# Column mean of an 8192x8192 matrix: 8 MB instead of 4 MB tiles, three quarters of the sums on VectorE, and all loads ahead of the outputs

## The chip, the cores and the metric

The kernel runs on one core of a Trainium2 chip; the other cores are idle. The metric is the time of one execution in microseconds (us), as the median of several runs. The profile's span, from the first to the last instruction, is about 1.8 us shorter than the time of the same run. Names of engines: PE is TensorE (matmul), DVE is VectorE, SP is SyncE; SPq is SP's queue, on which every DMA of this kernel is issued in program order.

## The reference

```python
def setup_inputs():
    return {"x": np.random.randn(8192, 8192).astype(np.float32)}

def reference(x):
    return np.mean(x, axis=0)
```

The input is 268.4 MB and is read once. The output is 32 KB.

## The kernel before

The matrix is read in 64 tiles of 128 rows (4 MB, one row of 32 KB per partition), in five buffers. PE sums over the partitions: a matmul with a column of 1/8192 as the stationary operand adds a block of 512 columns into a row of PSUM. The 16 blocks lie in six PSUM banks, three to a bank, at partitions 0, 32 and 64, so that matmuls of three blocks run side by side (in the trace 32 of them end within 7.0 us, though one takes 0.6 to 1.1 us). An f32 matmul is two instructions in the trace. In the last tile each bank is copied to SBUF by DVE and sent out, in the same loop that issues the loads:

```python
    for i in range(ntile):
        last = i == ntile - 1
        ...                      # pieces: head, bank by bank in the last two tiles, else whole
        t = in_pool.tile([P, C], fp32, name=f"in{i}", tag="in")
        for b0, nb in pieces:
            lo, hi = b0 * BLK, (b0 + nb) * BLK
            nc.sync.dma_start(out=t[:, lo:hi], in_=xt[i][:, lo:hi])
            for b in range(b0, b0 + nb):
                cols = slice(b * BLK, (b + 1) * BLK)
                mm(b, t[:, cols], stop=last)
            if last:
                ...
                nc.vector.tensor_copy(out=out_sb[0:rows, chunk], in_=ps[q][0:rows, :])
                ...
                nc.sync.dma_start(out=dst, in_=src)
```

Of the kernel before, what the change touches and what calls it, by code (L numbers as in the profile page):

```python
# [1 line left out]

# [4 lines left out]

BUFS = 5
GPB = 3  # L10
N_SPLIT = 2
HEAD_SPLIT = True
PROBE = False


@with_exitstack
def kernel(
    ctx: ExitStack,
    tc: tile.TileContext,
    x: bass.AP,  # L20
    out: bass.AP,
):
    nc = tc.nc
    P = nc.NUM_PARTITIONS
    R, C = x.shape
    fp32 = mybir.dt.float32
    BLK = 512
    nblk = (C + BLK - 1) // BLK
    assert C % BLK == 0 and R % P == 0
    inv_r = 1.0 / float(R)  # L30
    ntile = R // P
    nbank = (nblk + GPB - 1) // GPB

    pieces_bank = []
    b0 = 0
    for q in range(nbank):
        nb = min(GPB, nblk - b0)
        pieces_bank.append((b0, nb))
        b0 += nb
    pieces_head = [(0, 1), (1, nblk - 1)] if HEAD_SPLIT else [(0, nblk)]  # L40

    in_pool = ctx.enter_context(tc.tile_pool(name="in_pool", bufs=BUFS))
    const_pool = ctx.enter_context(tc.tile_pool(name="const_pool", bufs=1))
    out_pool = ctx.enter_context(tc.tile_pool(name="out_pool", bufs=1))
    psum_pool = ctx.enter_context(tc.tile_pool(name="psum_pool", bufs=1, space=bass.MemoryType.PSUM))

    ones = const_pool.tile([P, 1], fp32)
    nc.vector.memset(ones, inv_r)  # L48

    ps = [psum_pool.tile([P, BLK], fp32, name=f"ps{q}", tag=f"ps{q}") for q in range(nbank)]  # L50
    for q in range(nbank):
        rows = 32 * (min(GPB, nblk - q * GPB) - 1) + 1
        if rows > 1:
            nc.vector.memset(ps[q][0:rows], 0.0)  # L54
    out_sb = out_pool.tile([P, nbank * BLK], fp32)

    if PROBE and R >= 64 and C >= 4096:
        pr = const_pool.tile([64, 4096], fp32)
        nc.gpsimd.dma_start(out=pr[32:64, :], in_=x[0:32, 0:4096])

    def g_out(b):
        q, r = divmod(b, GPB)
        return ps[q][32 * r : 32 * r + 1, :]

    started = [False] * nblk

    def mm(b, rhs, stop=False):
        nc.tensor.matmul(g_out(b), ones, rhs, start=not started[b], stop=stop)  # L68
        started[b] = True

    xt = x.rearrange("(n p) m -> n p m", p=P)

    for i in range(ntile):
        last = i == ntile - 1
        if i == 0:
            pieces = pieces_head
        elif i >= ntile - N_SPLIT:
            pieces = pieces_bank
        else:
            pieces = [(0, nblk)]  # L80
        t = in_pool.tile([P, C], fp32, name=f"in{i}", tag="in")
        for b0, nb in pieces:
            lo, hi = b0 * BLK, (b0 + nb) * BLK
            nc.sync.dma_start(out=t[:, lo:hi], in_=xt[i][:, lo:hi])  # L84
            for b in range(b0, b0 + nb):
                cols = slice(b * BLK, (b + 1) * BLK)
                mm(b, t[:, cols], stop=last)
            if last:
                q = b0 // GPB
                rows = 32 * (nb - 1) + 1  # L90
                chunk = slice(q * BLK, (q + 1) * BLK)
                nc.vector.tensor_copy(out=out_sb[0:rows, chunk], in_=ps[q][0:rows, :])  # L92
                src = out_sb[0 : 32 * nb, chunk].rearrange("(r p) c -> r p c", p=32)[:, 0, :]
                dst = out[b0 * BLK : (b0 + nb) * BLK].rearrange("(r c) -> r c", c=BLK)
                nc.sync.dma_start(out=dst, in_=src)  # L95


# [1 line left out]
_INS = ['x']  # L99
_OUTS = [((8192,), 'float32')]  # L100


# [23 lines left out]
```

## Time and profile before

| | before |
|---|---|
| time, median of 5 runs | 639.2 us (639.1 to 640.9) |
| span of the profiled run | 638.3 us |
| 268.4 MB at the 431 GB/s of the middle | 623 us |
| PE busy | 427.9 us (67%) |
| DVE busy | 6.6 us (1%) |

The page of the kernel before: in 40 slices of the span, the busy share of the DMA engines in tenths and the GB/s they moved; then the DMA queue that fetches instructions (packets, MB, share).

```profile
DMA  9999999999999999999999999999999999999993
GB/s 372 446 430 427 426 427 435 443 431 426 429 429 426 435 436 431 432 429 429 426 433 432 432 437 426 433 424 433 431 434 433 426 435 427 432 431 434 417 388 132
q8 instruction: 16, 0.26, 0.2%
```

The DMA engines are full in every slice but the last, and the rate is flat near 430 GB/s until the last three slices. Sixteen packets of 16 KB fetch instructions while the kernel runs.

The table of windows of the kernel before: start and end of the window, its length, then busy us and instructions of each engine, the clock granted to PE, the DMA share and GB/s.

```profile
core 0: us, PE busy (x) PEld busy (x) DVE busy (x) POOL busy (x), PEclk, DMA share, GB/s
24.00:580.00 556.00, 377.79 (x1824) 67.65 (x1821) 0.00 (x0) 0.00 (x0) 0.85 1.00 431
624.30:638.30 14.00, 6.65 (x20) 0.38 (x20) 2.74 (x4) 0.00 (x0) 0.60 0.40 133
```

The first row says what bounds the kernel: DMA 100% busy at 431 GB/s, PE two thirds busy. The second is the end: DMA only 40% busy for 14 us. PE's timeline shows the same in the middle (start, length, instruction, and in brackets the idle time before it and what ended it):

```profile
325.39 7.01 PE L68 MATMUL ps<-in,ones 128*1 128x512 f32 x32 [2.71 <-DMA in<-in_x_dram]
335.10 5.31 PE L68 MATMUL ps<-in,ones 128*1 128x512 f32 x32 [2.70 <-DMA in<-in_x_dram]
```

A tile comes every 9.71 us, PE needs 5.3 to 8.1 us for it (the two lines show 7.0 and 5.3) and then waits for the next.

The end in SP's timeline and, in the last line, on PE (kernel before):

```profile
622.43 0.83 SPq L95 DMA_DIRECT2D out_dram<-out_sb  x1
623.31 0.36 SPq L84 DMA_DIRECT2D in<-in_x_dram  x1
624.26 2.52 SPq L95 DMA_DIRECT2D out_dram<-out_sb  x2
626.83 0.40 SPq L84 DMA_DIRECT2D in<-in_x_dram  x1
630.23 0.70 SPq L95 DMA_DIRECT2D out_dram<-out_sb  x1
630.98 0.40 SPq L84 DMA_DIRECT2D in<-in_x_dram  x1
633.84 2.77 SPq L95 DMA_DIRECT2D out_dram<-out_sb  x2
633.72 1.86 PE L68 MATMUL ps<-in,ones 128*1 128x512 f32 x2 [0.66 <-DMA in<-in_x_dram]
```

Outputs (L95) and loads (L84) alternate. An output waits for a copy, which waits for PE, which waits for a load; the next load stands behind it. The last three loads leave at 623.3, 626.8 and 631.0 us, and the DMA engines run dry between them.

### The profile page before, as it was taken

To read this page: it belongs to the slowest core of one execution; us is meant where nothing else is said; L and a number is where in the kernel's file an instruction comes from. 1 tells how busy PE (TensorE), PEld (TensorE's weight loads), DVE (VectorE), ACT (ScalarE), POOL (GpSimd) and SP (SyncE) were. 2 spreads that over 40 slices of the span, in tenths; PEclk is the share of its full clock that TensorE was granted. 3 is DMA by queue.
4 is the path that set the end of the run, shared out by engine and by line. 5 is a ranking of instruction groups with operands and counts; after the bars stand their busy time and mean duration, and the time that the engine had idled before them with its cause. 6 is when DMAs were issued, how large, how long until landed. Compare 5 with 4: busy or idle time off the path is not lost.

```text
span 638.3 us, 4305 instructions
## 1 busy us (share of the span) xinstructions
PE 427.9 (67%) x2048; PEld 75.6 (12%) x2048; DVE 6.6 (1%) x12; POOL 0.2 (0%) x4
## 2 busy tenths in 40 slices
PE   3676775866667667667667576677586666675884
PEld 0111110111111111101111011111011111110110
DVE  1000000000000000000000000000000000000002
POOL 0000000000000000000000000000000000000000
PEclk9878878787888898878887987887878788978886
DMA  9999999999999999999999999999999999999993
GB/s 372 446 430 427 426 427 435 443 431 426 429 429 426 435 436 431 432 429 429 426 433 432 432 437 426 433 424 433 431 434 433 426 435 427 432 431 434 417 388 132
DMA packets 10849, 268.74 MB, mean 421 GB/s; under 512 B 1216, under 2 KB 1216, under 8 KB 2896
## 3 DMA queue, kind: packets, MB, share of 16 engines
q1 hardware_dynamic: 10832, 268.47, 98.2%
q8 instruction: 16, 0.26, 0.2%
q14 instruction: 1, 0.01, 0.0%
HBM read 268.44 MB, written 0.03 MB: 421 GB/s over the span
## 4 chain that ended last, share of the span: by engine, by line
DMA 83%; PE 15%; SPq 0%; DVE 0%; issue 0%
DMA in<-in_x_dram 83%; PE ps L68 15%; DVE out_sb L92 0%; SPq L95 0%; SPq L84 0%
## 5 line engine op out<-in xcount | busy, mean ns | idle before, releaser
L68 PE MATMUL ps<-in,ones 128*1 128x512 f32 x2048 | 427.9, 730 | 207.7 <-DMA in<-in_x_dram 204.0
L68 PEld LDWEIGHTS ps<-in,ones 128*1 128x1 f32 x2048 | 75.6, 95 | 558.2 <-issue 284.7
L92 DVE COPY out_sb<-ps 65x512 f32<-65x512 f32 (+1 forms) x6 | 4.1, 685 | 628.6 <-PE ps L68 628.6
L54 DVE MEMSET ps<- 65x512 f32 x5 | 2.4, 485 | 0.3
L110 POOL MEMSET const-bfloat16-1.0<- 128x1 bf16 x1 | 0.1, 101 | 0.0
L110 POOL MEMSET const-uint8-127<- 128x1 uint8 x1 | 0.1, 101 | 0.0
L110 POOL MEMSET const-float32-0.0<- 128x1 f32 x1 | 0.1, 98 | 0.2 <-issue 0.2
L110 POOL MEMSET const-float32-1.0<- 128x1 f32 x1 | 0.1, 98 | 0.0
L48 DVE MEMSET ones<- 128x1 f32 x1 | 0.1, 59 | 0.8 <-PEq L110 0.8
## 6 DMA issues: line engine op xcount, KB each, us to landing
in<-in_x_dram SPq DMA_DIRECT2D x61, 4096.0 KB, 41.7
in<-in_x_dram SPq DMA_DIRECT2D x10, 768.0 KB, 9.1
in<-in_x_dram SPq DMA_DIRECT2D x1, 3840.0 KB, 11.8
in<-in_x_dram SPq DMA_DIRECT2D x3, 256.0 KB, 16.1
out_dram<-out_sb SPq DMA_DIRECT2D x5, 6.0 KB
out_dram<-out_sb SPq DMA_DIRECT2D x1, 2.0 KB
```

Source lines behind the costliest of these rows:

```text
L48: nc.vector.memset(ones, inv_r)
L54: nc.vector.memset(ps[q][0:rows], 0.0)
L68: nc.tensor.matmul(g_out(b), ones, rhs, start=not started[b], stop=stop)
L92: nc.vector.tensor_copy(out=out_sb[0:rows, chunk], in_=ps[q][0:rows, :])
L110: nc = _bacc.Bacc("TRN2", target_bir_lowering=False, num_devices=1)
```

## The change

The intent: read 8 MB per DMA, as two rows (64 KB, contiguous) per partition; let DVE add 12 of the 16 column blocks of tiles 0 to 28 into an accumulator, and PE only 4; fold the accumulator into PSUM before tile 29; and in the last tile issue every load before the first output. Two buffers of 8 MB replace five of 4 MB. The core of the diff, with cuts (some lines are joined or shortened):

```diff
-BUFS = 5
+BUFS = 2
 GPB = 3
-N_SPLIT = 2
+NPE = 4
+NEND = 3
+ROWS_PER_PART = 2
...
+    x3 = x.rearrange("(n p two) m -> n p (two m)", p=P, two=rpp)
...
+        if not endgame:
+            nc.sync.dma_start(out=t, in_=x3[i])
+            for h in range(rpp):
+                for b in range(npe):
+                    mm(b, t4[:, h, b * BLK : (b + 1) * BLK])
+            for h in range(rpp):
+                if ndve:
+                    nc.vector.tensor_tensor(out=acc, in0=acc,
+                        in1=t4[:, h, npe * BLK :], op=mybir.AluOpType.add)
+            continue
+        if i == ntile - nend and ndve:
+            for j in range(ndve):
+                mm(npe + j, acc[:, j * BLK : (j + 1) * BLK])
...
         for b0, nb in pieces:
             ...
-            nc.sync.dma_start(out=t[:, lo:hi], in_=xt[i][:, lo:hi])
+                nc.sync.dma_start(out=t4[:, :, lo:hi], in_=x4[i][:, :, lo:hi])
+        for b0, nb in pieces:
             for b in range(b0, b0 + nb):
+                for h in range(rpp):
+                    mm(b, t4[:, h, ...], stop=(last and h == rpp - 1))
+                if last:
+                    ...
+                        flush_bank(q)        # copy and output DMA
```

Tile 29 is still loaded whole; tiles 30 and 31 come in pieces of three blocks, the very last ones of two, one and one.

More of the change, by code (lines that the diff above doesn't have):

```diff
@@ L7 @@
 from concourse._compat import with_exitstack
-BUFS = 5
+BUFS = 2
 GPB = 3
-N_SPLIT = 2
-HEAD_SPLIT = True
-PROBE = False
+NPE = 4
+NEND = 3
+ROWS_PER_PART = 2
 @with_exitstack
@@ L27 @@
     BLK = 512
-    nblk = (C + BLK - 1) // BLK
-    assert C % BLK == 0 and R % P == 0
+    assert C % BLK == 0
+    nblk = C // BLK
     inv_r = 1.0 / float(R)
-    ntile = R // P
+    rpp = ROWS_PER_PART
+    TR = rpp * P
+    if R % TR != 0:
+        rpp = 1
+        TR = P
+    assert R % TR == 0
+    ntile = R // TR
     nbank = (nblk + GPB - 1) // GPB
+    npe = min(NPE, nblk)
+    ndve = nblk - npe
+    nend = min(NEND, ntile)
     pieces_bank = []
-    b0 = 0
     for q in range(nbank):
-        nb = min(GPB, nblk - b0)
-        pieces_bank.append((b0, nb))
-        b0 += nb
-    pieces_head = [(0, 1), (1, nblk - 1)] if HEAD_SPLIT else [(0, nblk)]
+        b0 = q * GPB
+        pieces_bank.append((b0, min(GPB, nblk - b0)))
+    pieces_last = []
+    for idx, (b0, nb) in enumerate(pieces_bank):
+        if idx >= len(pieces_bank) - 2 and nb > 1:
+            pieces_last.append((b0, nb - 1))
+            pieces_last.append((b0 + nb - 1, 1))
+        else:
+            pieces_last.append((b0, nb))
     in_pool = ctx.enter_context(tc.tile_pool(name="in_pool", bufs=BUFS))
     const_pool = ctx.enter_context(tc.tile_pool(name="const_pool", bufs=1))
-    out_pool = ctx.enter_context(tc.tile_pool(name="out_pool", bufs=1))
     psum_pool = ctx.enter_context(tc.tile_pool(name="psum_pool", bufs=1, space=bass.MemoryType.PSUM))
@@ L48 @@
     nc.vector.memset(ones, inv_r)
+    acc = None
+    if ndve:
+        acc = const_pool.tile([P, ndve * BLK], fp32)
+        nc.vector.memset(acc, 0.0)
+    out_sb = const_pool.tile([P, nbank * BLK], fp32)
     ps = [psum_pool.tile([P, BLK], fp32, name=f"ps{q}", tag=f"ps{q}") for q in range(nbank)]
@@ L54 @@
             nc.vector.memset(ps[q][0:rows], 0.0)
-    out_sb = out_pool.tile([P, nbank * BLK], fp32)
-    if PROBE and R >= 64 and C >= 4096:
-        pr = const_pool.tile([64, 4096], fp32)
-        nc.gpsimd.dma_start(out=pr[32:64, :], in_=x[0:32, 0:4096])
+    started = [False] * nblk
+    stopped_in_bank = [0] * nbank
     def g_out(b):
@@ L63, in g_out @@
         return ps[q][32 * r : 32 * r + 1, :]
-    started = [False] * nblk
     def mm(b, rhs, stop=False):
@@ L69, in mm, with flush_bank @@
         started[b] = True
-    xt = x.rearrange("(n p) m -> n p m", p=P)
-    for i in range(ntile):
+    def flush_bank(q):
+        ng = min(GPB, nblk - q * GPB)
+        rows = 32 * (ng - 1) + 1
+        chunk = slice(q * BLK, (q + 1) * BLK)
+        nc.vector.tensor_copy(out=out_sb[0:rows, chunk], in_=ps[q][0:rows, :])
+        b0 = q * GPB
+        src = out_sb[0 : 32 * ng, chunk].rearrange("(r p) c -> r p c", p=32)[:, 0, :]
+        dst = out[b0 * BLK : (b0 + ng) * BLK].rearrange("(r c) -> r c", c=BLK)
+        nc.sync.dma_start(out=dst, in_=src)
@@ new lines @@
+    x3 = x.rearrange("(n p two) m -> n p (two m)", p=P, two=rpp)
+    x4 = x.rearrange("(n p two) m -> n p two m", p=P, two=rpp)
+    for i in range(ntile):
+        t = in_pool.tile([P, rpp * C], fp32, name=f"in{i}", tag="in")
+        t4 = t.rearrange("p (two m) -> p two m", two=rpp)
+        endgame = i >= ntile - nend
+        if not endgame:
[4 more added lines that the diff above has]
+            for h in range(rpp):
+                if ndve:
+                    nc.vector.tensor_tensor(
+                        out=acc,
+                        in0=acc,
+                        in1=t4[:, h, npe * BLK :],
+                        op=mybir.AluOpType.add,
+                    )
+            continue
+        if i == ntile - nend and ndve:
+            for j in range(ndve):
+                mm(npe + j, acc[:, j * BLK : (j + 1) * BLK])
@@ L74 @@
         last = i == ntile - 1
-        if i == 0:
-            pieces = pieces_head
-        elif i >= ntile - N_SPLIT:
+        if i == ntile - nend and nend > 2:
+            pieces = [(0, nblk)]
+        elif not last:
             pieces = pieces_bank
         else:
-            pieces = [(0, nblk)]
-        t = in_pool.tile([P, C], fp32, name=f"in{i}", tag="in")
+            pieces = pieces_last
         for b0, nb in pieces:
             lo, hi = b0 * BLK, (b0 + nb) * BLK
-            nc.sync.dma_start(out=t[:, lo:hi], in_=xt[i][:, lo:hi])
-            for b in range(b0, b0 + nb):
-                cols = slice(b * BLK, (b + 1) * BLK)
-                mm(b, t[:, cols], stop=last)
-            if last:
-                q = b0 // GPB
-                rows = 32 * (nb - 1) + 1
-                chunk = slice(q * BLK, (q + 1) * BLK)
-                nc.vector.tensor_copy(out=out_sb[0:rows, chunk], in_=ps[q][0:rows, :])
-                src = out_sb[0 : 32 * nb, chunk].rearrange("(r p) c -> r p c", p=32)[:, 0, :]
-                dst = out[b0 * BLK : (b0 + nb) * BLK].rearrange("(r c) -> r c", c=BLK)
-                nc.sync.dma_start(out=dst, in_=src)
+            if (b0, nb) == (0, nblk):
+                nc.sync.dma_start(out=t, in_=x3[i])
+            elif rpp == 1:
+                nc.sync.dma_start(out=t4[:, 0, lo:hi], in_=x4[i][:, 0, lo:hi])
+            else:
+                nc.sync.dma_start(out=t4[:, :, lo:hi], in_=x4[i][:, :, lo:hi])
@@ L99 @@
+        for b0, nb in pieces:
+            for b in range(b0, b0 + nb):
+                for h in range(rpp):
+                    mm(b, t4[:, h, b * BLK : (b + 1) * BLK], stop=(last and h == rpp - 1))
+                if last:
+                    q = b // GPB
+                    stopped_in_bank[q] += 1
+                    if stopped_in_bank[q] == min(GPB, nblk - q * GPB):
+                        flush_bank(q)
 _INS = ['x']
```

## The prediction

> **What bounds it now.** The DMA stream. Table of windows: from 24 to 600 us the DMA engines are 100% busy at 431 GB/s, PE 392 of 576 us, DVE never. The Trainium skill ("DMA: Bandwidth & Descriptors", Where 436 GB/s comes from) puts the ceiling at 435 GB/s; the trace is at 99% of it. In the timeline PE starts a 4 MB tile every 9.71 us and needs 5.3 to 8.1 us for it; in the wait list it waits 204 us for input. 268.4 MB at 432 GB/s are 621 us of the 638.3 us span; some 17 us lie outside the stream, most after 600 us (slices 39 and 40 of the page: 388 and 132 GB/s).
>
> **What the change moves.**
> - 12 of 16 column blocks of tiles 0 to 28 go from PE to DVE, as f32 adds of 128x6144. The Trainium skill ("VectorE: DVE Perf Modes", the TRN2 errata) gives (N+151)/0.96 ns for them: estimate 6.56 us each, 13.1 us per 8 MB tile; no trace here shows one yet. PE was not on the critical path, so relieving it gains nothing by itself.
> - 5 buffers of 4 MB become 2 of 8 MB. A tile loads in 19.42 us; its buffer is free about 13.4 us after landing; issue to first packet is about 1 us. The next load is queued 4 to 5 us before the running one ends, so the stream should not break. This is the thinnest margin.
> - 64 KB instead of 32 KB rows per partition: at most 0.4% less packet cost. PE instructions fall from 2048 to about 700, so the 16 KB instruction fetches, which delay single DMA engines about 1 us each, become fewer: 1.5 to 2 us less at the end.
> - Head: one 8 MB load, no small piece: 0.8 us gained.
> - Tail, the real gain: output DMAs now stand between the input pieces on the one SP queue and wait there for PE and DVE (SP's waits: 18.6 us on the copy). The last pieces are issued at 623.3, 626.8 and 631.0 us and the last lands at 633.7; without these waits about 628.7. The change issues every input before the first output: 5 us gained.
> - Costs: two 8 MB tiles instead of two 4 MB go in pieces; 768 KB take 1.88 us against 1.82 at full rate: 0.7 us lost. The last block needs 4 instead of 2 dependent PE passes, 0.85 us each at the low clock: 1.7 us lost. In the last three tiles PE needs 10 (warm) to 17 us per 8 MB, still under 19.4.
>
> **Sum.** 638.3 - 5 - 0.8 - 2 - (0 to 2) + 0.7 + 1.7: about 632 us of span, a time of 633 us: 1% faster, inside 2%. Range 629 to 639. Faster by over 2%: 0.04; within 2%: 0.91; slower: 0.05.
>
> **What would show it.** DMA 100% and 431 GB/s in the middle; DVE adds of 6.5 us, busy about 380 us; PE starts tiles every 19.4 us; SP's waits in the middle are on DVE and end 4 to 6 us before the running load lands; in the tail no input issue behind an output, last input landing near 627, then about 6 us of passes, copy and output.
>
> **What would make it wrong.** Slower adds, or a longer way from the add's end to the next DMA's first packet: above 19.4 us in all, each tile adds a bubble, and 1 us of it costs about 30 us. 64 KB rows that read slower. PE cold in the last tiles and falling behind the pieces, which would give the tail's gain back.

## The result, and the profile after

The changed kernel takes 632.08 us (median of 7 runs, 631.86 to 632.34) beside 639.53 us for the kernel before (13 runs, 639.11 to 641.09). The ratio is 0.988, with a 95% interval of 0.987 to 0.989. The kernel is 1.2% faster; the predicted 633.0 us and its range of 629 to 639 us hold.

The page of the changed kernel, the same lines, and the group of the adds (busy us, mean ns of one, idle before):

```profile
GB/s 399 420 445 424 441 399 466 404 457 428 437 441 424 445 424 453 412 454 412 457 407 457 408 453 412 453 412 450 416 449 416 449 416 449 416 453 412 406 414 249
q8 instruction: 5, 0.08, 0.1%
L109 DVE TENSOR_TENSOR acc<-acc,in 128x6144 f32<-128x6144 f32 x58 | 380.4, 6558 | 188.8 <-DMA in<-in_x_dram 187.8
```

The last two slices moved 414 and 249 GB/s instead of 388 and 132. (The slices in the middle go up and down more than before. A 64 KB packet seems to be counted in one slice, so single slices say less here than the window below.) The add takes 6558 ns. The Trainium skill ("VectorE: DVE Perf Modes", the TRN2 errata) gives (N+151)/0.96 ns, checked there for 512 and 2048 elements; as an estimate, that is 6557 ns for 6144 elements, and the trace agrees.

The table of windows of the changed kernel:

```profile
24.00:580.00 556.00, 167.76 (x464) 23.67 (x463) 379.10 (x58) 0.00 (x0) 0.63 1.00 434
585.00:625.80 40.80, 31.31 (x190) 6.53 (x188) 2.75 (x4) 0.00 (x0) 1.00 0.98 398
```

In the middle the stream is as full as before, at 434 instead of 431 GB/s. PE's work has more than halved, and that is not where the time came from: PE was not the bound. The Trainium skill ("DMA: Bandwidth & Descriptors", Where 436 GB/s comes from) names 435 GB/s as the ceiling of the SBUF ports through which a core's DMA engines write; the trace comes within 0.3% of it. The same section lets a limit of about 358 GB/s on the HBM's side bind for loads from HBM; this trace, of one core with the others idle, lies well above that.

SP's timeline of the changed kernel, followed by the last matmuls on PE and the last add and copies on DVE:

```profile
579.31 30.97 SPq L135 DMA_DIRECT2D in<-in_x_dram  x13
612.14 16.63 SPq L93 DMA_DIRECT2D out_dram<-out_sb  x6
620.81 1.91 PE L82 MATMUL ps<-in,ones 128*1 128x512 f32 x12 [1.94 <-DMA in<-in_x_dram]
623.32 4.42 PE L82 MATMUL ps<-in,ones 128*1 128x512 f32 x16 [0.60 <-DMA in<-in_x_dram]
566.10 13.15 DVE L109 TENSOR_TENSOR acc<-acc,in 128x6144 f32<-128x6144 f32 x2 [6.20 <-DMA in<-in_x_dram]
627.78 0.68 DVE L89 COPY out_sb<-ps 1x512 f32<-1x512 f32 x1 [0.57 <-PE ps L82]
```

All 13 pieces are issued before the first output, and PE keeps up with them at the full clock.

Where the 7.9 us of the spans went can be booked from the records of semaphore updates, in which each load shows 16 updates. The profile counts 16 DMA engines, and I read one update as the end of one engine's share; the records do not name the engine. The table compares the same rows of the matrix, with the last of the 16 updates:

| us from the start of the span | before | after | difference gained |
|---|---|---|---|
| rows 0 to 255 landed | 22.69 | 22.63 | 0.06 |
| rows 0 to 7679 landed | 589.17 | 585.61 | 3.56 |
| last input landed | 633.68 | 625.82 | 7.86 |
| end of the span | 638.3 | 630.4 | 7.9 |

So 3.6 us come from the stream, 4.3 from the last two tiles, and nothing from what follows the last load (4.6 us in both). The 3.6 us of the stream fall in three. The first of the 16 updates for rows 0 to 255 comes 0.26 us earlier. From there it advances by 19.365 us per 8 MB instead of 19.425 (29 tiles: 1.7 us). And the last update trails the first by 1.99 us at row 7679 instead of 3.55 (1.6 us).

### The profile page after: what moved, and what is told of

The parts are those of the page before. It is cut to its first block, busy times and chain, and to the rows that moved or that the text cites. A ratio compares the mean times of both kernels' runs of the same rounds, so it can differ in the third digit from the quotient of the medians.

```text
span 630.4 us, 1591 instructions
## 1 busy us (share of the span) xinstructions
PE 207.2 (33%) x680; PEld 31.5 (5%) x680; DVE 392.1 (62%) x71; POOL 0.2 (0%) x4
## 4 chain that ended last, share of the span: by engine, by line
DMA 67%; DVE 29%; PE 2%; SPq 1%; issue 0%; DVEq 0%
DMA in<-in_x_dram 67%; DVE acc L109 29%; PE ps L82 2%; SPq L135 1%; SPq L103 0%; DVE out_sb L89 0%; DVEq L109 0%; SPq L131 0%
## 5 line engine op out<-in xcount | busy, mean ns | idle before, releaser
L109 DVE TENSOR_TENSOR acc<-acc,in 128x6144 f32<-128x6144 f32 x58 | 380.4, 6558 | 188.8 <-DMA in<-in_x_dram 187.8
L82 PE MATMUL ps<-in,ones 128*1 128x512 f32 x656 | 201.3, 858 | 413.0 <-DMA in<-in_x_dram 413.0
L82 PEld LDWEIGHTS ps<-in,ones 128*1 128x1 f32 x656 | 30.6, 95 | 582.7 <-DMA in<-in_x_dram 426.5
L82 PE MATMUL ps<-acc,ones 128*1 128x512 f32 x24 | 6.0, 912 | 7.5 <-DVE acc L109 7.5
L65 DVE MEMSET acc<- 128x6144 f32 x1 | 5.2, 5178 | 1.3 <-issue 1.3
## 6 DMA issues: line engine op xcount, KB each, us to landing
in<-in_x_dram SPq DMA_DIRECT2D x9, 1536.0 KB, 20.8
```

What stands on the lines that cost most here:

```text
L65: nc.vector.memset(acc, 0.0)
L82: nc.tensor.matmul(g_out(b), ones, rhs, start=not started[b], stop=stop)
L109: nc.vector.tensor_tensor(out=acc, in0=acc, in1=t4[:, h, npe * BLK :], op=mybir.AluOpType.add,)
```

## The experiments

Theory A, after these numbers: the gain has three parts that do not depend on PE's or DVE's speed. The order on SP's queue at the end gives most of it; fewer instruction fetches and fewer packets give about 1.6 us each. Rival B: PE relieved by DVE is the gain. Rival C: the large transfers as such are the gain. Afterwards a second question is tried, how thin the margin of the two buffers is.

### e1: the kernel before, with the last tile's loads issued first

```diff
+        if last:
+            for b0, nb in pieces:
+                lo, hi = b0 * BLK, (b0 + nb) * BLK
+                nc.sync.dma_start(out=t[:, lo:hi], in_=xt[i][:, lo:hi])
         for b0, nb in pieces:
             lo, hi = b0 * BLK, (b0 + nb) * BLK
-            nc.sync.dma_start(out=t[:, lo:hi], in_=xt[i][:, lo:hi])
+            if not last:
+                nc.sync.dma_start(out=t[:, lo:hi], in_=xt[i][:, lo:hi])
```

> The kernel before with one change: all loads of the last tile are issued ahead of its output DMAs. Theory A (the order on the SP queue in the tail is the largest part of the gain): the last load lands about 5 us earlier, near 628.7 instead of 633.7 us, so a ratio to before of 0.992 to 0.993, about 634.5 us. Rival B (what gains is PE relieved by DVE): nothing of that is in here, ratio 1.000. Rival C (what gains is the larger transfers): ratio 1.000 too.

Measured: 634.37 us beside 640.13 us, ratio 0.991 (0.989 to 0.993). SP's timeline of this run:

```profile
608.57 7.86 SPq L85 DMA_DIRECT2D in<-in_x_dram  x5
622.38 8.60 SPq L100 DMA_DIRECT2D out_dram<-out_sb  x6
```

The last input landed at 628.65 us, 5.03 us earlier than before, as the theory had it. A few lines moved in the old kernel give 5.8 us of the 7 to 8 us; with neither larger tiles nor DVE. B and C fall as explanations of the main part. (What follows the last load takes 4.0 us here instead of 4.6: the last two passes of PE start 0.43 us apart instead of 0.81.)

### e2: the changed kernel, with outputs between the loads again

```diff
-        for b0, nb in pieces:
+        def load(b0, nb):
             ...
+        if not last:
+            for b0, nb in pieces:
+                load(b0, nb)
         for b0, nb in pieces:
+            if last:
+                load(b0, nb)
```

> The changed kernel with one part undone: in the last tile each output DMA stands between the loads again. Theory A: 3 to 4.5 us slower than the changed kernel (632.1 us), about 636 us, ratio to before about 0.994; SP issues loads behind outputs and the last load lands 3 to 4.5 us later than 625.8 us. Rivals B and C: it stays at 632 to 633 us, ratio 0.988 to 0.990.

Measured: 638.25 us beside 640.13 us, ratio 0.997 (0.996 to 0.998), 6.2 us slower than the changed kernel; more than expected. SP's and PE's timelines show why:

```profile
617.18 1.20 SPq L135 DMA_DIRECT2D in<-in_x_dram  x2
624.73 0.72 SPq L93 DMA_DIRECT2D out_dram<-out_sb  x1
625.91 0.57 SPq L135 DMA_DIRECT2D in<-in_x_dram  x1
613.70 1.91 PE L82 MATMUL ps<-in,ones 128*1 128x512 f32 x12 [1.81 <-DMA in<-in_x_dram]
620.34 3.60 PE L82 MATMUL ps<-in,ones 128*1 128x512 f32 x12 [4.74 <-DMA in<-in_x_dram]
```

The table of windows for the slow piece (its seventh column is the clock granted to PE):

```profile
620.00:624.00 4.00, 3.60 (x12) 0.43 (x12) 0.00 (x0) 0.00 (x0) 0.50 1.02 422
```

The wait for a late load is followed by a slow piece on PE, 3.60 us instead of 1.91 for the same 12 instructions, at half the clock. That delays the copy, the output behind it, and the next load. My expectation had costed the waits with PE at the full clock. The order of the queue is thus confirmed from the other side: without it the changed kernel keeps only 0.3%.

### e3: the changed kernel, all blocks on PE, and e5: single-column matmuls added

```diff
-NPE = 4
+NPE = 16
```

> The changed kernel with all 16 blocks on PE and none on DVE, all else alike. Theory A: relieving PE bought only fewer instruction fetches; with 2048 matmuls again there are about 16 fetches of 16 KB instead of 5, and the landings end about 1.5 us later: 633 to 634 us, ratio 0.990 to 0.991. Rival B (the offload is the gain): most of the gain is lost, 636 to 640 us, ratio 0.995 to 1.000.

Measured: 633.73 us, ratio 0.990 (0.989 to 0.992). Taking DVE out costs 1.65 us of the 7.5. To tell PE's work from PE's number of instructions, e5 keeps the adds on DVE and adds short matmuls whose result nobody reads:

```diff
+            for _ in range(24):
+                nc.tensor.matmul(dummy[96:97, 0:1], ones, t4[:, 0, 0:1], start=True, stop=True)
```

> The changed kernel plus 24 matmuls of a single column per 8 MB tile, into a row of PSUM that nobody reads: as many PE instructions as with all blocks on PE (2048 or more) but hardly more PE work, and the adds stay on DVE. Theory A (what the offload buys is fewer instruction fetches): fetches rise from 5 to about 16, landings spread to about 3.5 us again, 633.5 to 634 us, like the kernel with all blocks on PE (633.7). Rival D (what the all-PE kernel lost is PE's work, not its instructions): 632.1 us, unchanged.

Measured: 633.67 us beside 639.26 us, ratio 0.991 (0.990 to 0.992), the same as e3. The pages of e3 and e5, PE's busy time and the instruction queue, e3 first:

```profile
PE 400.6 (63%) x2048; PEld 73.0 (12%) x2048; DVE 6.6 (1%) x12; POOL 0.2 (0%) x4
q8 instruction: 16, 0.26, 0.2%
```

```profile
PE 222.9 (35%) x2072; PEld 69.1 (11%) x2072; DVE 392.1 (62%) x71; POOL 0.2 (0%) x4
q8 instruction: 16, 0.26, 0.2%
```

PE is busy 401 us in one and 223 us in the other, yet both have 16 fetches of 16 KB and the same time, and in both the last update of the load of row 7679 trails the first by more than 3 us (3.58 and 3.17, against 1.99 with 5 fetches). So the offload to DVE is worth 1.65 us because it removes instructions, not work. The Trainium skill ("Runtime: NRT & Kernel Launch", Instruction fetch mechanics) says that instructions come in blocks of 16 KB, 256 instructions each; the traces agree if the fetches of this queue are PE's: its 4096 instructions before are 16.0 such blocks and its 1360 after are 5.3, beside 16 and 5 fetches. A fetch takes about 1.05 us in the DMA records, and its cost shows as one or a few of the 16 updates coming later from then on. That the fetch delays that one DMA engine is the reading that fits; the records do not name the engine.

### e4: the changed kernel with 4 MB tiles in four buffers

```diff
-BUFS = 2
+BUFS = 4
-NEND = 3
-ROWS_PER_PART = 2
+NEND = 5
+ROWS_PER_PART = 1
```

> The changed kernel with 32 KB rows: tiles of 4 MB in 4 buffers instead of 8 MB in 2, the same share in pieces at the end. Theory A: twice as many packets, each with about 7 ns of its own, cost 0.06 us per 8 MB, 1.7 us in all: 633.5 to 634 us, ratio 0.990 to 0.991. Rival C (the large transfers are the gain): 636 us or more, ratio 0.995 or more. If four buffers were better than two for the stream, it would come out below 632 us.

Measured: 633.78 us, ratio 0.990 (0.989 to 0.992), 1.7 us slower than the changed kernel, as expected. The middle of this run, beside the 434 GB/s of the changed kernel:

```profile
24.00:580.00 556.00, 201.05 (x460) 20.16 (x457) 374.73 (x58) 0.00 (x0) 0.61 1.00 432
```

The first of the 16 updates advances by 19.428 us per 8 MB, as before the change (19.425), instead of 19.365. (The 7 ns of the expectation are these 0.06 us over the 8 packets of 64 KB that each of 16 engines moves per 8 MB, if they share evenly.) The number of fetches (5) and the spread at row 7679 (1.97 us) stay as in the changed kernel, so the two parts of the stream's gain are separate. The larger transfers are worth about 1.7 us and no more; this run also has more buffers and smaller pieces at the end, but row 7679, ahead of those pieces, already landed 1.97 us later than in the changed kernel.

Added up, e1 (5.8 us), e3 (1.65) and e4 (1.7) come to more than the 7.5 us. Two costs of the changed kernel go against them: its pieces, cut from two tiles of 8 MB instead of two of 4 MB (0.9 us between e11, below, and e12) and four passes of PE after the last load instead of two (4.6 us from the last landing to the end, 4.0 in e1). The changed kernel itself was run in two calls, with 632.08 and 632.03 us; e3, e4 and e5 were run in other calls and are compared with it across calls.

### e6 to e10: how thin the margin of two buffers is

With two buffers, the load after the next can only be issued when DVE has finished with the tile. In the changed kernel that is 13.3 us after the tile landed, 6.05 us before the running load of 19.36 us ends. e6 puts all 16 blocks on DVE; the others keep NPE at 4 and add one more add per tile, which reads the tile and whose result nobody uses:

```diff
-NPE = 4
+NPE = 0
```

```diff
+            nc.vector.tensor_tensor(out=extra, in0=t[:, 0:EXTRA],
+                in1=t[:, EXTRA : 2 * EXTRA], op=mybir.AluOpType.add)
             continue
```

EXTRA is 5120 in e7, 5632 in e8, 3904 in e9 and 2432 in e10. The estimates of the adds' times in the expectations use the formula of the errata quoted above; the traces have 8.69 us for 128x8192 (e6), 5.48 for 128x5120 (e7), 6.02 for 128x5632 (e8) and 2.68 for 128x2432 (e10).

> The changed kernel with all 16 blocks on DVE for tiles 0 to 28: two adds of 128x8192, estimate (8192+151)/0.96 = 8.69 us each, so a buffer is free 17.5 us after landing and, with about 1.1 us from there to the first packet, 0.8 us before the running load ends. Theory A: the stream still does not break, 631.5 to 634 us. If the way from add to packet is longer than I think, it breaks and the time is above 635 us.

> The changed kernel plus one more add per tile on DVE (128x5120, estimate 5.5 us) that reads the tile: its buffer is free about 18.8 us after landing, the next packets come at 19.85 us, 0.5 us after the running load of 19.36 us has ended. My prediction's rule (each us over costs 1 us in every tile, about 30 us in all): about 646 us. Rival E (with two buffers two tiles share one such lateness, so the period is half of load + work + latency): half of that, about 639 us.

> As the run before with a longer extra add (128x5632, estimate 6.0 us): free 19.3 us after landing, packets at 20.4 us, 1.0 us late. My prediction's rule: about 661 us. Rival E: about 647 us. DVE alone (19.2 us per tile) is still below the load's 19.36 us, so DVE's throughput is not the limit in either.

> The changed kernel plus one add of 128x3904 per tile (estimate 4.2 us), so that the buffer is free 17.5 us after landing, as with all blocks on DVE (671.6 us), but with 4 blocks still on PE. If the lead of the next load decides (1.9 us before the running load ends, too short because a load issued to drained queues lands 21.8 us after its issue instead of 19.36), this run is slow too: the simple rule, half of (19.36 + 17.5 + 2.5) per tile, gives about 642 us; if an issue close to the end of the running load is worse than a late one, as the all-DVE run suggests, 660 to 672 us. If the all-DVE kernel was slow for another reason (wide adds, no PE work), this one is near 632 us.

> The same with an extra add of 128x2432 (estimate 2.7 us): free 16 us after landing, the next load issued 3.4 us before the running one ends. If about 2.5 us of lead are needed, the stream does not break: 632 to 634 us. If more is needed because the fast DMA engines end 2 us ahead of the slowest, some of it is lost: 636 to 650 us.

Measured, in order of the lead. The time from a tile's landing to the issue on SP is read from the traces; the lead is 19.36 us minus that, so what the lead would be if the running load kept its pace (where the stream breaks, a load takes longer, and the next one has more). DVE is busy at most 19.1 us per tile, less than the load takes, in all of them.

| run | landing to issue, us | lead, us | time, us | ratio to before (95%) | GB/s from 24 to 580 us |
|---|---|---|---|---|---|
| changed kernel (e12) | 13.3 | 6.05 | 632.0 | 0.987 (0.986 to 0.989) | 434 |
| e10 | 15.8 | 3.6 | 648.5 | 1.012 (1.010 to 1.014) | 421 |
| e9 | 17.3 | 2.0 | 665.1 | 1.039 (1.036 to 1.043) | 411 |
| e6, all on DVE | 17.5 | 1.8 | 671.6 | 1.050 (1.048 to 1.053) | 408 |
| e7 | 18.6 | 0.8 | 667.2 | 1.044 (1.042 to 1.046) | 411 |
| e8 | 19.1 | 0.2 | 671.7 | 1.051 (1.049 to 1.053) | 406 |

The table of windows, for e6 and for e10:

```profile
24.00:580.00 556.00, 0.00 (x0) 0.00 (x0) 468.83 (x55) 0.00 (x0) 1.00 0.97 408
```

```profile
24.00:580.00 556.00, 158.82 (x445) 22.57 (x441) 436.42 (x84) 0.00 (x0) 0.63 0.99 421
```

DVE's timeline, the starts of three tiles in e10, and two in e7:

```profile
301.80 6.56 DVE L111 TENSOR_TENSOR acc<-acc,in 128x6144 f32<-128x6144 f32 x1 [4.63 <-DMA in<-in_x_dram]
...
321.18 6.56 DVE L111 TENSOR_TENSOR acc<-acc,in 128x6144 f32<-128x6144 f32 x1 [3.76 <-DMA in<-in_x_dram]
...
341.56 6.56 DVE L111 TENSOR_TENSOR acc<-acc,in 128x6144 f32<-128x6144 f32 x1 [4.75 <-DMA in<-in_x_dram]
```

```profile
329.01 6.56 DVE L111 TENSOR_TENSOR acc<-acc,in 128x6144 f32<-128x6144 f32 x1 [1.41 <-DMA in<-in_x_dram]
...
349.81 6.56 DVE L111 TENSOR_TENSOR acc<-acc,in 128x6144 f32<-128x6144 f32 x1 [2.37 <-DMA in<-in_x_dram]
```

In e10 DVE still idles about 4 us before each tile, so it is no bound, yet of these tiles one comes after 19.38 us and the next after 20.38. In e7 the two starts are 20.8 us apart, and the landings of its 29 steps average 20.3 us.

What follows. The stream breaks long before the lead reaches the 1 us that I had taken as the way from issue to first packet. It breaks already at a lead of 3.6 us. Two things seen in the traces fit that; no run separates them. First, the 16 updates of a load do not come together: in the changed kernel the first comes 1.7 us before the last, so the engine that ends first needs the next work earlier than the lead says. e5 speaks for this: at tiles 22 to 27 its loads were issued 6.05 us before the last update of the running load but only 2.8 us before the first, and the first updates still advanced by 19.36 us per load. In e10 the issue came 0.9 to 3.3 us before the first update, and these advanced by 19.9 us. Second, a load that finds the queues drained lands about 21.8 us after its issue instead of taking 19.36 (e7, issued at 204.77, 0.8 us before the load ahead of it landed, landed at 226.61): 2.5 us on top. The first 16 packets of that load took 2.7 to 3.5 us each, about 3.05 in the middle, instead of 2.42. The Trainium skill ("DMA: Bandwidth & Descriptors", Anatomy of one DMA) puts the fixed cost of a DMA near 2.0 us, for DMAs issued from GpSimd; these loads from SP show 2.5.

Neither of my rules for the size held. The prediction's rule gave 646 us for e7 and 661 us for e8 (measured 667.2 and 671.7), rival E gave 639 and 647. Rival E has some support in the slope: between e7 and e8 the wait grew by 0.5 us and the medians by 4.5 us (the profiled spans by 8.5), nearer to half than to the whole of 0.5 us in 29 tiles (7 or 15 us); but the runs of e7 alone lie up to 5.0 us apart. Its level is wrong, and e9 and e6, with more lead than e7, are no faster than e7, which no rule of mine gives. In e6 a load issued at 287.87, 1.8 us before the previous one had fully landed, had its first packets spread from 1.0 to 3.1 us after the issue; in e7, with a shorter lead, from 0.95 to 1.8 us. A load issued while some engines still work seems to be handed out more slowly. The runs do not settle that: the records name no DMA engine, and I put the packets together by their times.

### e11: fewer pieces at the end, and e12: the changed kernel again

```diff
-NEND = 3
+NEND = 2
...
+    pieces_last = [(0, 6), (6, 6), (12, 2), (14, 1), (15, 1)]
...
-        if i == ntile - nend and nend > 2:
+        if not last:
             pieces = [(0, nblk)]
-        elif not last:
-            pieces = pieces_bank
```

> The changed kernel with fewer and wider pieces at the end: tile 30 is loaded whole and only the last tile in pieces of 6, 6, 2, 1 and 1 blocks. Pieces of 3 blocks ran at 1536 KB in 3.77 us against 3.63 at full rate; this should give 1.1 us back: about 631 us, 0.2% faster than the changed kernel in the same call.

> The changed kernel again, unchanged, as the yardstick for the other runs of this call on the same chip: 632.1 us, ratio to before 0.988.

Measured: e11 631.10 us (630.89 to 631.32), ratio 0.986 (0.984 to 0.987); e12 632.03 us (631.90 to 632.16), ratio 0.987 (0.986 to 0.989). The ranges of the runs do not overlap: 0.9 us or 0.15% faster, 1.1 expected. e11 is the fastest kernel, by a small step. (NEND = 2 also moves the fold by one tile, so that DVE adds tiles 0 to 29; the two are not separated.)

## Why the prediction was right

- "The DMA stream" bounds the kernel, and "relieving it [PE] gains nothing by itself": right. The window of the middle shows 434 GB/s with PE at 168 of 556 us; e3 and e5 show that the offload gives 1.65 us through instructions alone, whether PE works 401 or 223 us.
- "Tail, the real gain", 5 us less 0.7 for the pieces: right, and shown. Last two tiles: 4.3 us gained. e1 alone: last landing 5.03 us earlier. e2: 6.2 us lost when undone, of which part goes with PE's lower clock (0.50 from 620 to 624 us).
- Packets, "0 to 2 us": 1.7 us, by e4 and by the period of 19.365 instead of 19.425 us.
- Fetches, "1.5 to 2 us": 1.6 us, by e3 and e5.
- "Head ... 0.8 us gained": wrong. The first 8 MB landed 0.06 us earlier, by the first of the 16 updates 0.26.
- The last block's "4 instead of 2 dependent PE passes, 0.85 us each at the low clock: 1.7 us lost": wrong. The passes started 0.43 us apart, since PE ran at the full clock (1.00 in the window up to 625.8 us, against 0.60 in the last 14 us before), and what follows the last load takes 4.6 us in both kernels. Why the clock was higher was not tested. What the traces show is that PE idled at most 1.94 us between the last pieces here, and 2.24 us before its first slow piece in the kernel before (4.74 us in e2). This miss and that of the head have opposite signs and cancel in part (1.7 against 0.8 us), which was luck for the sum.
- "1 us of it costs about 30 us", and a way of 1 us from issue to first packet as the measure of the margin: wrong. The stream did not break (the predicted lead of "4 to 6 us" was 6.05), so the predicted time did not suffer, but e10 shows that 2.5 us more work per tile would have made the changed kernel slower than the one before (648.5 us). I had costed a margin of 4 to 5 us against a need of 1 us; the need is more than 3.6 us.

## What to carry to other kernels

In a kernel bound by loads, look first at what shares the loads' queue: an output that waits there for a result holds back every load behind it, and moving the issues costs nothing. Moving work to an idle engine gains little while the stream is full; ask instead how early the next load can be issued, and leave several us of lead (6 us sufficed here, 3.6 did not). By the reading above the lead has to cover the spread of the DMA engines as well as the start of a load. Four buffers of half the size cost 1.7 us here and have far more lead than two large ones: in e4 a load was issued at 545.71 us and the load ahead of it landed at 568.13, 22.4 us later.

## What the Trainium skill lacked or had wrong

- "DMA: Bandwidth & Descriptors" gives a fixed cost per DMA, but not how early a load must be issued for back-to-back loads to stay gapless. With loads of 8 MB in two buffers, a lead of 6.05 us kept 434 GB/s, 3.6 us gave 421 GB/s, 2 us and less 406 to 411 GB/s (changed kernel, e10, e9, e6 to e8).
- "DMA: Bandwidth & Descriptors", Anatomy of one DMA: about 2.0 us of fixed cost, fitted to DMAs from GpSimd. An 8 MB load from SP into drained queues landed 21.8 us after its issue, 2.5 us more than the 19.36 us that each load takes in a gapless stream (e7).
- "Runtime: NRT & Kernel Launch", Instruction fetch mechanics, calls the cost of crossing a 16 KB boundary mostly hidden; what a fetch costs a full DMA stream stands on no page. Sixteen instead of five fetches of 16 KB, about 1.05 us each, cost 1.6 us of 632 (e3, e5).
- "VectorE: DVE Perf Modes", Zero memsets, says that a memset takes one cycle per element; at the page's 0.96 GHz that is, as an estimate, 6.4 us for 128x6144 elements. The changed kernel's trace shows 5178 ns.
